# Moving two thirds of one layer's modulation from TensorE matmuls to VectorE row sums

## The chip, the cores and the metric

The kernel runs on one core of a Trainium2 chip. The metric is the device time of one execution in microseconds (us); smaller is better. Engines are named as in the profile: PE is TensorE's matmul (PEld its weight loads), DVE is VectorE, ACT is ScalarE, POOL is GpSimd, SP is SyncE, which here issues most of the DMAs.

## The reference

Two small models run one after the other on 256 tokens of width 1024. The first has two layers (convolution, pooling mixer, sparse attention, gated output). The second takes its output as a latent sequence x, adds a context sequence xc of 256 tokens, and has two layers of mixers (gated linear attention, short convolution, neighbourhood attention) and a convolutional FFN. Each layer of the second model is modulated by vectors that depend on the conditioning vectors c and c_ctx alone:

```python
for layer in range(DEPTH):                       # DEPTH = 2
    mod = silu(c) @ w_ada[layer] + b_ada[layer]        # 6 x 1024 values for the latent
    sh1, sc1, g1, sh2, sc2, g2 = split(mod, 6)
    modc = silu(c_ctx) @ w_ada[layer] + b_ada[layer]   # and 6 x 1024 for the context
    ...
    u = (rmsnorm(x) * (1 + sc1) + sh1) @ w_in[layer]
    x = x + g1 * (mixers(u) @ w_out[layer])
    h = rmsnorm(x) * (1 + sc2) + sh2
    x = x + g2 * conv_ffn(h)
    ...
```

The context goes the same way in layer 0, with modc; in layer 1 only its input to the mixers is needed. All is f32. A layer's w_ada has 1024 x 6144 values, 24 MB; nothing but c and c_ctx is needed to use it, so this product can be done at any time before its sixths are used.

## The kernel before, in words

Activations lie feature-major: 128 features on the partitions, tokens along the free axis. Weights come as units of 128 x 1024 f32 (512 KB), loaded by SP in the order of their use (`rawunit`, L425) into 4 buffers. `unit` (L437 and L445) splits a unit into a high and a low part, the high one by a copy on ACT, the low one by a subtraction on DVE, into 4 buffers, and `mm3` (L384 to L386) makes each product in three matmuls. `ftile` (L381 with `raw` operands) is the plain f32 form that some tiles take. A product's sum lies in one of 3 PSUM banks called mm; short chains (attention, norms, scans) use 4 banks called ax, and one bank is called ada.

The program is written as a main line of such tiles. Side work is written as Python generators: `tick` calls them, so that the main line's tiles and the side work's instructions alternate in program order, and a scheduler of the framework then fixes each engine's order, by program order and what is ready in its own model. A tick also calls `feed`, which takes `pace` steps of one more generator, `s.fill`. That is where the modulation is done:

- **`ada(0)`**, layer 0, inside the first model's layer 0: six rounds (a sixth of the 6144 columns each) of eight steps. A step loads 512 KB of w_ada into one of 4 buffers (L630) and issues four f32 matmuls with a stationary operand of 32 columns (silu of c and c_ctx in the first two), one for each quarter of the bank's partitions. Each shows as two instructions, so that one step is a group of 8 in the trace. At the end of a round ACT copies the bank out, and `turn` transposes it on PE (L619) and adds the bias on DVE. 48 steps and 6 turns, one step per tick.
- **`ada_rows(1)`**, layer 1, inside layer 0's FFN of the second model: c and c_ctx are spread over the partitions (one DMA of 1 MB, L651) and put through silu; then for each of 48 blocks of 128 features a load of 512 KB of the transposed w_ada into one of 2 buffers (L661) and a multiply-and-sum along the row on DVE (L664) with a read of its accumulator into `mod`. Blocks 0 to 15 are summed for context (j = 1) and latent (j = 0), blocks 16 to 47 for the latent only: 3 steps of preparation and 64 row sums, at 1.7 steps for each FFN pair (PAIR_PACE) and 2.5 for each tile of the down projection.

`mod[i]` has 48 columns per layer: 0 to 15 are sh1 and sc1, 16 to 23 g1, 24 to 39 sh2 and sc2, 40 to 47 g2. `norm2` uses columns 0 to 15 before the mixers and 24 to 39 before the FFN; `residual` uses 16 to 23 after the mixers and 40 to 47 after the FFN.

Order of the second model's layer 0 (`layer2`): `norm2` of latent and context; `mixers` (projections with the scan's and the attention's side work between them, then the output projection in three loops of 8 tiles: the part from scan and convolution for all tokens, then the attention's part for the context, then for the latent, with `norm2` for the FFN behind each of the last two); `ffn` (13 pairs of up projections, first half of the down projection, 9 pairs, second half). In layer 0's mixers before, `s.fill` is empty.

Of the kernel before, what the change touches and what calls it, by code (L numbers as in the profile page):

```python
# [8 lines left out]
F32 = mybir.dt.float32  # L9
# [14 lines left out]
PAIR_PACE = 1.7  # L24
# [16 lines left out]
ADA_PIN = 48  # L41
# [275 lines left out]
def layout(a):  # L317
    a = {k: np.asarray(v) for k, v in a.items()}
    d = {}
    units = []  # L320
    sp1 = []
    tokb = []
    for i in range(DEPTH):
        units += block1_units(i, a)
        sp1.append(block1_small(i, a))
        tokb.append(np.concatenate([a["b_in"][i][TOKC], a["b_in"][i][rng(V, 512)]]))
    d["units1"] = np.stack(units)
    d["sp1"] = np.stack(sp1)
    d["sw1"] = np.stack([block1_small_w(i, a) for i in range(DEPTH)])
    d["tokb"] = np.stack(tokb)  # L330
    d["xT"] = fm(a["x"][0].T, rng(0, T))
    d["pT"] = np.stack([fm(a["p"][i, 0].T, rng(0, T)) for i in range(DEPTH)])
    d["units2"] = np.stack([u for i in range(DEPTH) for u in block2_units(i, a)])
    d["sp2"] = np.stack([block2_small(i, a) for i in range(DEPTH)])
    d["wg2"] = np.stack([gate_weights(i, a) for i in range(DEPTH)])
    d["nab"] = np.stack([na_bias(i, a) for i in range(DEPTH)])
    d["wada"] = a["w_ada_2"][0].reshape(8, 128, 6144)

    d["wadaT"] = a["w_ada_2"][1].T.reshape(48, 128, 1024)
    d["crow"] = np.stack([a["c_2"][0], a["c_ctx_2"]]).reshape(1, 2 * D)  # L340
    d["cc"] = np.stack([colvec(a["c_2"][0]), colvec(a["c_ctx_2"])], 2).reshape(128, 16)
    d["ctxT"] = fm(a["ctx_2"][0].T, rng(0, T))
    d["c2"] = consts2()
    d["c0"] = consts0()
    d["c1"] = consts1()
    return {k: np.ascontiguousarray(v) for k, v in d.items()}
# [3 lines left out]
class Prog:  # L350
    def __init__(s, ctx, tc, A, out, dbg=None):
# [12 lines left out]
        s.turns = False  # L364
        s.inner = 0
# [242 lines left out]
    def ada(s, i):  # L608
        nc, A = s.nc, s.A
        pool = s.tmp  # L610
        mod = s.const.tile([128, 48, 2], F32, name=s.nm("mod"), tag=f"mod{i}")
        s.mod.append(mod)
# [13 lines left out]
        for rd in range(6):  # L626
            ps = bank[:, rd % 2 * 256 : rd % 2 * 256 + 256]
            for k in range(KT):
                w = s.t([128, 1024], "wada", 4, pool=pool)
                (s.pin if rd * KT + k < ADA_PIN else lambda x: x)(nc.sync.dma_start(w, A["wada"][k, :, rd * 1024 : rd * 1024 + 1024]))  # L630
# [14 lines left out]
    def ada_rows(s, i, bufs, pool):  # L645
        nc, A = s.nc, s.A
        mod = s.const.tile([128, 48, 2], F32, name=s.nm("mod"), tag=f"mod{i}")
        s.mod.append(mod)
        bias = s.sp2[i]["ada"]
# [3 lines left out]
        th = s.t([128, D], "adaj", 1, pool=pool)  # L653
        for j in range(2):
            s.a(th, c[:, j], AF.Tanh, scale=0.5)
# [3 lines left out]
        for m in range(48):  # L659
            w = s.t([128, D], "wada", bufs, pool=pool)  # L660
            s.pin(nc.sync.dma_start(w, A["wadaT"][m]))  # L661
            for j in (1, 0) if m < 16 else (0,):
                out = s.t([128, D], "adaj", 1, pool=pool) if j else w
                nc.vector.tensor_tensor_reduce(out=out, in0=w, in1=c[:, j], scale=1.0, scalar=bias[:, m : m + 1],  # L664
                                               op0=ALU.mult, op1=ALU.add, accum_out=mod[:, m, j : j + 1])
                yield 0

# [543 lines left out]
    def ffn(s, i, both, c0, n):  # L1211
# [28 lines left out]
        if both:  # L1240
            s.fill, s.pace = s.ada_rows(i + 1, 2, s.mx), PAIR_PACE
# [54 lines left out]
    def mixers(s, i, both, c0, n):  # L1296
# [3 lines left out]

        v = s.big([128, 4, 384], "A")
# [109 lines left out]
        st = [{}, {}]  # L1411
        for m in range(KT):
            s.residual(i, m, wtile(range(5), 0, m, c0, n), 16, c0, n, st, False)
            s.tick(NA_TICK)
        for j in (1, 0) if both else (0,):
# [12 lines left out]
            if both:  # L1428
                s.norm2(i, 1, s.rows(st[j]), j)
# [322 lines left out]
```

## Time and profile before

| | us |
|---|---|
| median of 3 runs (range) | 1469.65 (1467.91 to 1471.45) |
| the profiled execution | 1469.05 |
| its span, first to last instruction | 1467.2 |
| PE busy in it | 1403.8 (96%) |
| PEld busy | 1196.6 (82%) |
| DVE busy | 1057.1 (72%) |
| ACT busy | 695.6 (47%) |
| POOL busy | 160.3 (11%) |

The mean granted TensorE clock is 0.979 of full speed. The profiled execution lies 1.85 us above its own span and 0.6 us below the median of the runs. Layer 0 of the first model fills the span up to about 242 us and layer 1 up to about 420; the second model's layer 0 has its mixers from about 430 to 687 us and its FFN from there to about 1085; layer 1 fills the rest. A share of busy time is a mean over these stages, so each stage is read by itself: which engine has no idle time in it, and what ends the waits of the engines that do. A row of idle time says who released the engine; idle time of an engine that isn't the bound costs nothing.

### The profile page before, as it was taken

To read this page: it belongs to the slowest core of one execution; us is meant where nothing else is said; L and a number is where in the kernel's file an instruction comes from. 1 tells how busy PE (TensorE), PEld (TensorE's weight loads), DVE (VectorE), ACT (ScalarE), POOL (GpSimd) and SP (SyncE) were. 2 spreads that over 40 slices of the span, in tenths; PEclk is the share of its full clock that TensorE was granted. 3 is DMA by queue.
4 is the path that set the end of the run, shared out by engine and by line. 5 is a ranking of instruction groups with operands and counts; after the bars stand their busy time and mean duration, and the time that the engine had idled before them with its cause. 6 is when DMAs were issued, how large, how long until landed. Compare 5 with 4: busy or idle time off the path is not lost.

```text
span 1467.2 us, 25799 instructions
## 1 busy us (share of the span) xinstructions
PE 1403.8 (96%) x10178; PEld 1196.6 (82%) x10178; DVE 1057.1 (72%) x2128; ACT 695.6 (47%) x1294; POOL 160.3 (11%) x176
## 2 busy tenths in 40 slices
PE   8889999689999999999999999999999999999997
PEld 7657688677997877768888888888898887999997
DVE  6895656996976655465898886787367665698694
ACT  4635655636765233454444422343246245476562
POOL 1840001920020000002100000000210000100001
PEclk9999999999999999999999999999999999999998
DMA  7677685343452211112353565555333233376662
GB/s 263 249 254 263 206 310 187 101 144 115 135 172 86 88 59 55 58 55 101 89 183 117 164 223 201 171 186 174 89 97 101 87 97 92 108 211 195 185 197 77
DMA packets 63761, 218.02 MB, mean 149 GB/s; under 512 B 7254, under 2 KB 12312, under 8 KB 63512
## 3 DMA queue, kind: packets, MB, share of 16 engines
q1 hardware_dynamic: 58224, 208.17, 44.7%
q10 hardware_dynamic: 5416, 8.20, 1.8%
q8 instruction: 80, 1.31, 0.4%
q14 instruction: 41, 0.34, 0.1%
HBM read 215.30 MB, written 1.05 MB: 147 GB/s over the span
## 4 chain that ended last, share of the span: by engine, by line
PE 79%; DVE 9%; POOL 4%; issue 3%; ACT 3%; DMA 2%; ACTq 0%; POOLq 0%; DVEq 0%; SPq 0%
PE mm L384 21%; PE mm L385 21%; PE mm L386 21%; PE ax L381 10%; DVE hl L445 3%; POOL acc L943 2%; PE mm L381 2%; PE ada L381 2%; DMA raw<-in_units_dram 1%; DVE acc L392 1%; PE ax L1705 1%; ACT hl L437 1%; POOL sqa L526 1%; DVE isc L392 1%; DVE xx L392 1%
## 5 line engine op out<-in xcount | busy, mean ns | idle before, releaser
L384 PE MATMUL mm<-xx,hl 128*128 128x256 f32 (+1 forms) x1720 | 557.9, 326 | 16.2 <-ACT qr L405 7.6
L386 PE MATMUL mm<-xx,hl 128*128 128x256 f32 (+1 forms) x1720 | 549.0, 320 | 4.9 <-DVE hl L445 4.9
L385 PE MATMUL mm<-xx,hl 128*128 128x256 f32 (+1 forms) x1720 | 549.7, 320 | 0.0
L445 DVE TENSOR_TENSOR hl<-raw,hl 128x1024 fp32r<-128x1024 f32 x286 | 359.2, 1256 | 107.4 <-ACT hl L437 104.2
L437 ACT ACTIVATE hl<-raw 128x1024 fp32r<-128x1024 f32 x286 | 301.0, 1054 | 172.9 <-PE mm L386 151.3
L384 PEld LDWEIGHTS mm<-xx,hl 128*128 128x128 f32 x1720 | 328.4, 191 | 60.5 <-issue 13.1
L386 PEld LDWEIGHTS mm<-xx,hl 128*128 128x128 f32 x1720 | 328.7, 191 | 32.2 <-DVE hl L445 6.3
L385 PEld LDWEIGHTS mm<-xx,hl 128*128 128x128 f32 x1720 | 328.9, 192 | 29.7 <-issue 6.3
L392 DVE SCALAR_TENSOR_TENSOR y<-mm,sp,y 128x255 f32<-128x255 f32 (+1 forms) x184 | 109.1, 595 | 25.8 <-ACT y L405 24.3
L384 PE MATMUL mm<-hid,hl 128*128 128x256 f32 (+1 forms) x374 | 123.0, 329 | 0.0
L385 PE MATMUL mm<-hid,hl 128*128 128x256 f32 (+1 forms) x374 | 123.0, 329 | 0.0
L386 PE MATMUL mm<-hid,hl 128*128 128x256 f32 (+1 forms) x374 | 122.7, 328 | 0.0
L405 ACT ACTIVATE y<-mm,sp 128x256 f32<-128x256 f32 (+1 forms) x92 | 60.4, 657 | 116.2 <-PE mm L386 116.0
L526 POOL TENSOR_TENSOR sqa<-sqa,sq 128x256 f32<-128x256 f32 x36 | 32.1, 896 | 690.5 <-ACT sq L405 689.8
L384 PEld LDWEIGHTS mm<-hid,hl 128*128 128x128 f32 x374 | 70.5, 188 | 7.2
L385 PEld LDWEIGHTS mm<-hid,hl 128*128 128x128 f32 x374 | 70.5, 188 | 7.1
L386 PEld LDWEIGHTS mm<-hid,hl 128*128 128x128 f32 x374 | 70.5, 188 | 6.9
L392 DVE SCALAR_TENSOR_TENSOR x<-mm,mod,x 128x256 f32<-128x256 f32 x96 | 43.5, 478 | 44.2 <-PE mm L386 44.0
L385 PE MATMUL mm<-hl,xx 128*128 128x416 f32 (+3 forms) x192 | 68.4, 356 | 5.2 <-DVE hl L445 5.2
L664 DVE CUSTOM_DVE_ANT_0 wada<-wada,crow,sp 128x1024 f32<-128x1024 f32 x48 | 61.0, 1280 | 11.1 <-DMA wada<-in_wadaT_dram 10.8
L384 PE MATMUL mm<-hl,xx 128*128 128x416 f32 (+3 forms) x192 | 68.1, 356 | 0.4 <-DVE glr L1306 0.2
L386 PE MATMUL mm<-hl,xx 128*128 128x416 f32 (+3 forms) x192 | 67.1, 350 | 0.0
(279 smaller groups left out, 1752.1 us busy)
## 6 DMA issues: line engine op xcount, KB each, us to landing
raw<-in_units_dram SPq DMA_DIRECT2D x296, 512.0 KB, 3.7
wada<-in_wada_dram SPq DMA_DIRECT2D x48, 512.0 KB, 4.9
wada<-in_wadaT_dram SPq DMA_DIRECT2D x48, 512.0 KB, 4.6
nab<-in_nab_dram ACTq DMA_DIRECT2D x12, 192.0 KB, 2.5
x<-in_xT_dram SPq DMA_DIRECT2D x4, 256.0 KB, 5.2
x<-in_ctxT_dram ACTq DMA_DIRECT2D x1, 1024.0 KB, 6.6
crow<-in_crow_dram SPq DMA_DIRECT2D x1, 1024.0 KB, 6.6
c<-in_c_dram ACTq DMA_DIRECT2D x1, 928.0 KB, 5.2
```

The source lines that it names most:

```text
L381: return s.nc.tensor.matmul(out, lhsT, rhs, start=start, stop=stop, **kw)
L384: s.nc.tensor.matmul(out, l[0], r[0], start=start, stop=False)
L385: s.nc.tensor.matmul(out, l[0], r[1], start=False, stop=False)
L386: s.nc.tensor.matmul(out, l[1], r[0], start=False, stop=stop)
L392: s.nc.vector.scalar_tensor_tensor(out, a, sc, b, op0, op1)
L405: s.nc.scalar.activation(out, in_, func, bias=bias, scale=scale)
L437: a = nc.scalar.activation(hl[:, 0], raw, AF.Copy)
L445: b = nc.vector.tensor_sub(hl[:, 1], raw, hl[:, 0].bitcast(F32))
L526: (eng or s.nc.vector).tensor_tensor(st["acc"], st["acc"], sq, ALU.add)
L664: nc.vector.tensor_tensor_reduce(out=out, in0=w, in1=c[:, j], scale=1.0, scalar=bias[:, m : m + 1], op0=ALU.mult, op1=ALU.add, accum_out=m ...
L943: nc.gpsimd.tensor_tensor(acc[:, j], acc[:, j], pr, ALU.add)
L1705: nc.tensor.transpose(pt[:, kt * 128 : kt * 128 + 128], L[j][:, kt * 128 : kt * 128 + 128], s.ident)
```

## The change

`ada(0)` keeps its first two rounds (sh1 and sc1, `ADA_PE = 2`): 16 steps and 2 turns stay on PE in the first model, 32 steps and 4 turns go. `ada_rows` takes a list of (layer, block) and is used twice. In layer 0's mixers it does blocks 16 to 39 of layer 0, for context and latent, at 0.8 steps per tick (3 steps of preparation, 48 row sums). In layer 0's FFN it does blocks 40 to 47 of layer 0 and then the 48 blocks of layer 1 (3 steps and 80 row sums), at 2.0 steps per pair. Before the output projection the generator is run on until g1 is there; before `norm2` for the FFN it is run to its end. A context row sum (j = 1) is now two instructions of 512 columns that write their products to the PSUM bank ada, the second starting from the first one's sum, so that no SBUF buffer is needed for them. A context row sum is one step, as before. The DMA scratch setting at the foot makes room in SBUF.

```diff
-PAIR_PACE = 1.7
+PAIR_PACE = 2.0
...
-ADA_PIN = 48
+ADA_PE = 2
+ADA_MIX = range(16, 40)
+MIX_PACE = 0.8
...
-    d["wada"] = a["w_ada_2"][0].reshape(8, 128, 6144)
-
-    d["wadaT"] = a["w_ada_2"][1].T.reshape(48, 128, 1024)
+
+    d["wada"] = a["w_ada_2"][0][:, : ADA_PE * 1024].reshape(8, 128, ADA_PE * 1024)
+    d["wadaT"] = a["w_ada_2"].transpose(0, 2, 1).reshape(DEPTH, 48, 128, 1024)
...
-        for rd in range(6):
+        for rd in range(ADA_PE):
...
-                (s.pin if rd * KT + k < ADA_PIN else lambda x: x)(nc.sync.dma_start(w, A["wada"][k, :, rd * 1024 : rd * 1024 + 1024]))
+                s.pin(nc.sync.dma_start(w, A["wada"][k, :, rd * 1024 : rd * 1024 + 1024]))
...
-    def ada_rows(s, i, bufs, pool):
+    def ada_rows(s, todo, bufs, pool):
...
-        th = s.t([128, D], "adaj", 1, pool=pool)
         for j in range(2):
+            th = s.t([128, D], "wada", bufs, pool=pool)
...
-        for m in range(48):
+        for i, m in todo:
+            mod, bias = s.mod[i], s.sp2[i]["ada"]
             w = s.t([128, D], "wada", bufs, pool=pool)
-            s.pin(nc.sync.dma_start(w, A["wadaT"][m]))
-            for j in (1, 0) if m < 16 else (0,):
-                out = s.t([128, D], "adaj", 1, pool=pool) if j else w
-                nc.vector.tensor_tensor_reduce(out=out, in0=w, in1=c[:, j], scale=1.0, scalar=bias[:, m : m + 1],
-                                               op0=ALU.mult, op1=ALU.add, accum_out=mod[:, m, j : j + 1])
+            s.pin(nc.sync.dma_start(w, A["wadaT"][i, m]))
+            for j in (1, 0) if m < 16 or i < DEPTH - 1 else (0,):
+                if j:
+
+                    out, b = s.bank("ada"), bias[:, m : m + 1]
+                    for h in range(2):
+                        c_ = slice(h * 512, h * 512 + 512)
+                        nc.vector.tensor_tensor_reduce(out=out, in0=w[:, c_], in1=c[:, j, c_], scale=1.0, scalar=b,
+                                                       op0=ALU.mult, op1=ALU.add, accum_out=mod[:, m, j : j + 1])
+                        b = mod[:, m, j : j + 1]
+                else:
+                    nc.vector.tensor_tensor_reduce(out=w, in0=w, in1=c[:, j], scale=1.0, scalar=bias[:, m : m + 1],
+                                                   op0=ALU.mult, op1=ALU.add, accum_out=mod[:, m, j : j + 1])
                 yield 0
+            if (i, m) == (0, 23):
+                s.gated = True
...
         if both:
-            s.fill, s.pace = s.ada_rows(i + 1, 2, s.mx), PAIR_PACE
+            s.fill = s.ada_rows([(0, m) for m in range(40, 48)] + [(1, m) for m in range(48)], 2, s.mx)
+            s.pace = PAIR_PACE
...
+        if both:
+            s.fill, s.pace = s.ada_rows([(0, m) for m in ADA_MIX], 2, s.mx), MIX_PACE
         v = s.big([128, 4, 384], "A")
...
         st = [{}, {}]
+        while both and not s.gated:
+            next(s.fill)
         for m in range(KT):
             s.residual(i, m, wtile(range(5), 0, m, c0, n), 16, c0, n, st, False)
             s.tick(NA_TICK)
+        s.pace = MIX_PACE
...
             if both:
+                for _ in s.fill:
+                    pass
                 s.norm2(i, 1, s.rows(st[j]), j)
...
-    nc = _bacc.Bacc("TRN2", target_bir_lowering=False, num_devices=1)
+    nc = _bacc.Bacc("TRN2", target_bir_lowering=False, num_devices=1, dynamic_dma_scratch_size=1024)
```

## Rows read from the trace of the kernel before

**Rows 1.** The page: busy time by engine, the chain that ended last.

```profile
PE 1403.8 (96%) x10178; PEld 1196.6 (82%) x10178; DVE 1057.1 (72%) x2128; ACT 695.6 (47%) x1294; POOL 160.3 (11%) x176
PE 79%; DVE 9%; POOL 4%; issue 3%; ACT 3%; DMA 2%; ACTq 0%; POOLq 0%; DVEq 0%; SPq 0%
```

**Rows 2.** The chain that ended last, 107 to 242 us: shares by line.

```profile
by line: PE mm L384 18.1%; PE mm L385 15.8%; PE mm L386 15.6%; PE ada L381 15.0%; PE ax L381 14.2%; PE mm L381 10.1%; PE ax L1094 2.5%; PE ax L384 2.5%; PE ax L385 1.4%; PE ax L386 1.4%; PE ax L619 1.1%; ACT aPT L405 0.7%; POOL clr L508 0.6
```

**Rows 3.** Busy time by window: length, PE, PEld, DVE, ACT, POOL; clock, DMA.

```profile
107.00:242.00 135.00, 133.54 (x1121) 105.28 (x1122) 81.12 (x200) 71.28 (x164) 1.63 (x2) 1.00 0.73 243
173.00:190.00 17.00, 17.00 (x162) 12.51 (x163) 10.96 (x22) 7.03 (x13) 0.00 (x0) 1.00 0.78 258
```

**Rows 4.** Groups by line, 107 to 242 us, PE: the modulation's matmuls and transposes.

```profile
L381 PE MATMUL ada<-wada,cs 128*32 128x256 f32 x280 | 22.8, 391 | 0.0
...
L619 PE MATMUL ax<-c,adae 128*128 128x128 f32 x8 | 1.8, 301 | 0.0
```

**Rows 5.** Timeline of PE around single steps of the modulation (start, duration).

```profile
154.06 0.64 PE L381 MATMUL ada<-wada,cs 128*32 128x256 f32 x8
154.63 0.44 PE L1094 MATMUL ax<-c,aL 128*128 128x128 f32 x2
...
190.86 0.28 PE L385 MATMUL mm<-xx,hl 128*128 128x256 f32 x1
190.97 0.28 PE L386 MATMUL mm<-xx,hl 128*128 128x256 f32 x1
191.18 0.64 PE L381 MATMUL ada<-wada,cs 128*32 128x256 f32 x8
191.75 0.39 PE L384 MATMUL ax<-qi,hl 128*128 128x256 f32 x1
191.98 0.28 PE L385 MATMUL ax<-acc,hl 128*128 128x256 f32 x1
```

**Rows 6.** Groups by line and form, DVE: row sums, preparation, a 512-column form on PSUM.

```profile
L664 DVE CUSTOM_DVE_ANT_0 wada<-wada,crow,sp 128x1024 f32<-128x1024 f32 x48 | 61.0, 1280 | 11.1 <-DMA wada<-in_wadaT_dram 10.8
...
L664 DVE DVE_READ_ACCUMULATOR2_ANT mod<- 128x1 f32 x64 | 5.2, 82 | 0.0
...
L392 DVE SCALAR_TENSOR_TENSOR crow<-adaj,crow 128x1024 f32<-128x1024 f32 x2 | 2.8, 1382 | 0.9 <-ACT crow L405 0.7
...
L401 DVE TENSOR_TENSOR scp<-mm,slO 128x512 f32<-128x512 f32 x2 | 1.4, 690 | 4.7 <-PE mm L386 4.7
```

**Rows 7.** Busy time by window, layer 0's mixers, their end, the FFN's beginning.

```profile
430.00:626.00 196.00, 193.70 (x1691) 154.12 (x1692) 113.49 (x301) 80.56 (x166) 10.02 (x11) 0.97 0.24 70
626.00:687.00 61.00, 58.26 (x341) 43.34 (x341) 34.67 (x89) 29.46 (x74) 5.30 (x6) 0.98 0.28 93
687.00:705.00 18.00, 14.86 (x90) 14.03 (x91) 13.39 (x29) 8.99 (x18) 5.41 (x7) 0.78 0.00 1
705.00:722.00 17.00, 15.54 (x120) 15.21 (x120) 14.63 (x33) 7.58 (x17) 1.62 (x1) 0.90 0.33 94
```

**Rows 8.** Waits of PE in the mixers, 430 to 668 us: total, times, longest.

```profile
PE ax L1621 <- DVE slO L401: 1.5, 1, 1.5
PE ax L1705 <- DVE slA L396: 1.1, 2, 0.5
```

**Rows 9.** Timeline of DVE at the context's norm, 691 to 694 us.

```profile
691.02 0.87 DVE L392 SCALAR_TENSOR_TENSOR nf<-x,modA,ax 128x256 f32<-128x256 f32 x2 [1.22 <-PE ax L381]
...
692.30 1.27 DVE L664 CUSTOM_DVE_ANT_0 adaj<-wada,crow,sp 128x1024 f32<-128x1024 f32 x1
```

**Rows 10.** The page, DMA issues: count, KB each, median us to landing.

```profile
wada<-in_wadaT_dram SPq DMA_DIRECT2D x48, 512.0 KB, 4.6
```

**Rows 11.** Busy time by window, layer 0's FFN: pairs of the first half, then the rest.

```profile
722.00:850.00 128.00, 128.00 (x584) 104.73 (x584) 115.20 (x168) 55.54 (x74) 0.00 (x0) 1.00 0.50 156
850.00:1050.00 200.00, 200.00 (x859) 161.33 (x858) 141.45 (x202) 66.58 (x83) 5.11 (x6) 1.00 0.55 179
```

**Rows 12.** Busy time by window, the tile ada alone, sum over 107 to 242 us.

```profile
sum 135.00, PE 22.78 PEld 5.75 ACT 1.88; mean PE 4.56 PEld 1.15 ACT 0.38
```

More of the change, by code (lines that the diff above doesn't have):

```diff
@@ L364, in __init__ @@
         s.turns = False
+        s.gated = False
         s.inner = 0
@@ L610, in ada @@
         pool = s.tmp
-        mod = s.const.tile([128, 48, 2], F32, name=s.nm("mod"), tag=f"mod{i}")
-        s.mod.append(mod)
+        for d in range(DEPTH):
+            s.mod.append(s.const.tile([128, 48, 2], F32, name=s.nm("mod"), tag=f"mod{d}"))
+        mod = s.mod[i]
         bias = s.sp2[i]["ada"]
@@ L641, in ada @@
         turn(*prev)
-    def ada_rows(s, i, bufs, pool):
+    def ada_rows(s, todo, bufs, pool):
         nc, A = s.nc, s.A
-        mod = s.const.tile([128, 48, 2], F32, name=s.nm("mod"), tag=f"mod{i}")
-        s.mod.append(mod)
-        bias = s.sp2[i]["ada"]
         c = s.t([128, 2, D], "crow", 1, pool=pool)
```

## The prediction, made before the changed kernel was run

> **What bounds the kernel now.** I read the page first. PE is busy for 96% of the span, DVE for 72%, and 79% of the chain that ended last runs on PE [rows 1]. A mean over stages decides nothing, so I went to the stage that loses work and then to the one that gains it.
>
> The stage that loses is layer 0 of the first model, 107 to 242 us. Before 107 us 13 of the 48 steps have run; the first 16 stay, so 32 of the 35 steps in this stretch go. Here PE is busy 133.5 of 135 us at the full clock (1.00, that is 2.4 GHz), DVE 81 and ACT 71 [rows 3]. The chain runs through PE almost wholly, and 15.0% of it, 20.2 us, are the modulation's matmuls, 1.1% its transposes [rows 2]. So PE is the bound here and these steps lie on its path.
>
> The stage that gains is layer 0's mixers and FFN. From 430 to 626 us PE is busy 193.7 of 196 us and DVE 113.5 [rows 7]; all that PE waits for DVE up to 668 us is 2.6 us [rows 8]. In the FFN's first pairs PE has no idle time and DVE is already busy 115.2 of 128 us [rows 11]. PE is the bound again, and DVE has room that differs by stretch.
>
> **What leaves PE.** 280 instructions are 35 groups of 8, 22.8 us busy [rows 4]. A busy time of overlapping matmuls is no price, so I take starts. Between split matmuls the last one starts at 190.97, the group at 191.18, the next at 191.75 and the one behind it at 191.98: 0.78 and 0.23 where two usual spacings are 0.11 each [rows 5], so a group costs 0.67 + 0.12 = 0.79. Between other f32 matmuls only the 0.57 from 154.06 to 154.63 counts [rows 5]. I put 20 groups at 0.79 and 12 (the attention's stretch and the layer's end) at 0.57: 15.8 + 6.8 = 22.6 us. Four turns with two transposes each, 1.8 us busy for four [rows 4], give 1.5 more. Together 24 us, the most there is to win. Not all of it will come: from 173 to 190 us eight groups leave 17.0 − 8 × 0.79 = 10.7 us of PE work beside 10.96 of DVE [rows 3], so DVE binds there next, and in the attention the chain over ACT and DVE shows. I take off 3: **−21 us**, with 20 to 24 as bounds (20 is the chain's own figure). The four copies on ACT, eight small additions on DVE and 32 loads on SP that go with them free nothing that binds here; they only bring the units' loads earlier.
>
> There is a rule that speaks against this reading. In this stretch the weight loads fill only 105.3 of the 135 us [rows 3]. The Trainium skill, Perfetto Trace Analysis, section Identifying the Most-Contended Engine, says that a matmul's busy share is a bad measure of how near PE is to its limit and that the share of the weight loads should be taken. By that PE would stand at 78% here and would not be the bound, and the sum below would begin with −5 in place of −21. The starts do not agree with it: they follow each other without a gap, and the group's 0.79 us is a spacing [rows 5]. I go by the starts and keep a PE that isn't the bound as a rival.
>
> **What comes to DVE.** A latent row sum is 1.28 us and its accumulator read 0.08 [rows 6]: 1.36. The trace has no row sum of 512 columns that writes to PSUM. Its bounds are half of the long form, 0.64, and no gain from the shortening, 1.28; I take 0.69, the 512-column form with an operand in PSUM [rows 6], which is nearest in size and memory. Two halves and two reads are 1.54, a block with both sums 2.90.
>
> - Mixers: 24 blocks, 69.6 us, and two preparations of 1.38 [rows 6] on DVE: 72.4 us. ACT gets four passes more of about a us each in a stretch where it is busy 80.6 of 196 us [rows 7], hidden. The upper bound of the half adds 48 × 0.59 = 28 us.
> - FFN: 8 blocks, 23.2, and 16 context sums of layer 1 that are now halves, 16 × 0.18 = 2.9: 26.1 us.
>
> **What of it shows.** Where do the steps fall? Counted in the code, layer 0's mixers have 36 ticks ahead of the output projection, then 8, 8 and 8. At 0.8 a tick that is 28 steps by the beginning of the output projection, which I put at 626 us, 13 more in the two loops that follow, and the last 10 of the 51 at one go before the context's `norm2`.
>
> - Up to 626 us: 3 steps of preparation and 25 of 1.45 us on the mean, 39 us into 82.5 us of idle DVE [rows 7]. DVE goes from 58 to 78%. At 90% it still costs PE nothing in the FFN's pairs [rows 11], which gives a lower bound of 0; but the scan's and the attention's chains alternate between PE and DVE, and each can wait for a row sum that has just begun. In the one short stretch with DVE at 86% and chains of norms, PE lost 1.5 of 17 us [rows 7], 9%, which makes 17 us of 196: the upper bound. Between the two I take the value near the FFN and near the 2.6 us that PE waits now [rows 8]: **+3 us**.
> - 626 to 687 us: 23 steps, 33.4 us, into 26.3 us of idle DVE [rows 7]: 7.1 us too much. What is queued behind it: columns 24 to 39 must be there before `norm2` of the context, which began about 691.0 us [rows 9], and the FFN's first tiles wait for that. Some of it will be done earlier, since a row sum needs only its load, and SP runs ahead: the first row sum of layer 1 ran at 692.3 [rows 9], long before the third pair's tick, where the code has it. The lower bound is 0. The upper bound is that nothing runs ahead: five blocks at one go through two buffers, each 4.6 us to land [rows 10] and 2.9 to sum, 5 × 7.5 / 2 = 19 us. I take **+5 us**.
> - SP: 24 loads and the 1 MB of c now stand among the units' loads, and one that waits for its buffer holds the units behind it. Eight units (four raw, four split) cover that, and the DMA engines are busy 24% there [rows 7]: 0. If that cover is gone, PE waits for a unit, which counts in the 17 us above. POOL's queue is passed by nothing.
> - FFN: at 2.0 steps a pair in place of 1.7 the first pairs get some 5 sums more and 14 split ones, 6.8 + 2.5 = 9.3 us into 12.8 idle [rows 11]; the rest has 58.6 idle. **+1 us**, bounds 0 and 9.
>
> Sum: −21 + 3 + 5 + 1 = −12. The profiled execution took 1469.05 us, 1.85 more than its span and 0.6 less than the median of the runs; 1469.05 − 12 = **1457 us**. With 20 to 24 won and 3 to 18 given back the case's own range is 1447 to 1467.
>
> **The rivals.**
>
> - *All row sums hidden.* For it: no idle PE at 90% DVE in the pairs [rows 11]. Against it: the 7.1 us too much before the FFN. 1469 − 24 = 1445.
> - *The norm's gate.* The last five blocks run at one go, the FFN starts 19 us later: −21 + 19 + 4 = +2, 1471. For it: the loop that empties the generator right ahead of `norm2`, PE already short there (14.9 of 18 us, 1.5 of 17 lost behind it) [rows 7]. Against it: the row sum at 692.3 [rows 9].
> - *DVE's order becomes the bound in the mixers.* A row sum cannot be interrupted; if half of the 72 us stand in front of a scan or attention step that PE waits for, the mixers grow by 36 us: 1469 − 21 + 36 + 1 = 1485. It decides from 20 us on, 28% of the row sums' time. Against it: 82.5 us of idle DVE up to 626 and three mm banks that feed PE meanwhile; for it: what PE waits for now are just such steps, the scan's sum and the attention's scaling [rows 8].
> - *PE was not the bound in the first model.* Then what goes is only the weight loads' share. The stretch has 35 steps with 5.75 us of these loads [rows 12]; 32 of them are 5.3 us: 1469 − 5 + 9 = 1473. Against it: the chain and the starts [rows 2, 5]. The Trainium skill, Perfetto Trace Analysis, section Identifying the Most-Contended Engine, is the rule that would lead here.
>
> That the change doesn't do what it says can hardly be: the 32 groups are out of the code.
>
> **How the numbers follow.** A measurement of this kernel can tell about 0.2%, 2.9 us. Chances: forecast 0.66, all hidden 0.14, the norm's gate 0.08, DVE's order 0.07, PE not the bound 0.05. Faster: 0.66 + 0.14 = 0.80; same: 0.08; slower: 0.07 + 0.05 = 0.12. The range takes in the forecast's own, the hidden case at 1445 and the gate at 1471, and leaves out 0.12 and a part of the forecast's tail.
>
> **What would show it.** Right: layer 0 of the first model ends 20 to 24 us earlier, at about 221 us, and layer 1 is shifted whole; 16 groups of modulation matmuls on PE; the halves at 0.69 us; DVE near 80% up to the output projection, PE's waits for DVE up by 3 us there; 5 us more between the last context tile and the FFN's first pairs. Wrong: an idle PE in 107 to 221 us with DMA or DVE as the releaser; PE waits for DVE of more than 20 us in the mixers, or a lower granted clock there; `norm2` of the context later than the shift allows by 10 us and more.

## The result, and the profile after

The changed kernel takes 1458.59 us (median of 4 runs, 1456.47 to 1459.71), the kernel before 1470.55 us on the same chip (4 runs, 1467.91 to 1474.62): a ratio of 0.9915, 95% interval 0.9888 to 0.9941. That is faster by more than the 0.2% that can be told, and 1.6 us above the forecast of 1457. The profiled execution took 1457.7 us with a span of 1455.9 us, against 1469.05 and 1467.2.

The page of the changed kernel, busy time by engine and the chain that ended last, answers to [rows 1]:

```profile
PE 1395.0 (96%) x9914; PEld 1197.0 (82%) x9914; DVE 1142.1 (78%) x2346; ACT 696.3 (48%) x1294; POOL 164.1 (11%) x176
PE 74%; DVE 11%; POOL 4%; issue 4%; DMA 3%; ACT 3%; ACTq 0%; POOLq 0%; DVEq 0%; SPq 0%
```

PE has lost 264 matmuls and DVE has 85 us more to do. PE is still busy for 96% of a shorter span. The groups by line and form, the modulation's matmuls and the row sums (count, busy us, mean ns), answer to [rows 4, 6]:

```profile
L384 PE MATMUL ada<-wada,cs 128*32 128x256 f32 x128 | 10.7, 406 | 5.1 <-ACT adae L408 5.1
...
L674 DVE CUSTOM_DVE_ANT_0 wada<-wada,crow,sp 128x1024 f32<-128x1024 f32 x80 | 101.8, 1280 | 5.4 <-DMA wada<-in_wadaT_dram 4.8
L670 DVE CUSTOM_DVE_ANT_0 ada<-wada,crow,mod 128x512 f32<-128x512 f32 x48 | 36.2, 754 | 0.7
L670 DVE CUSTOM_DVE_ANT_0 ada<-wada,crow,sp 128x512 f32<-128x512 f32 x48 | 36.1, 752 | 3.6 <-DMA wada<-in_wadaT_dram 3.3
L670 DVE DVE_READ_ACCUMULATOR2_ANT mod<- 128x1 f32 x96 | 13.2, 138 | 0.1
```

128 matmuls, 16 groups, are left. A half row sum into PSUM takes 0.75 us and its read 0.14.

Busy time by window of the changed kernel (length; PE, PEld, DVE, ACT, POOL busy with counts; granted clock, DMA share, GB/s), cut where about the same work stands (to within 2 us), answers to [rows 3, 7, 11]:

```profile
107.00:222.00 115.00, 114.45 (x893) 101.33 (x892) 80.62 (x194) 69.52 (x159) 1.79 (x2) 1.00 0.45 142
410.00:616.70 206.70, 203.59 (x1692) 160.96 (x1693) 158.09 (x405) 83.97 (x170) 11.30 (x11) 0.93 0.33 112
616.70:678.30 61.60, 60.65 (x350) 43.84 (x349) 53.24 (x133) 29.38 (x75) 5.09 (x6) 1.00 0.42 135
690.30:708.80 18.50, 13.87 (x81) 13.46 (x82) 15.96 (x36) 6.68 (x16) 1.62 (x1) 0.73 0.28 86
708.80:841.20 132.40, 132.40 (x618) 108.26 (x617) 125.74 (x213) 56.84 (x77) 0.00 (x0) 1.00 0.49 159
```

The first line is where the time comes from: 115 us for what took 135. The second is where it goes: the mixers up to the output projection took 196 us before. DVE stands at 76% there, near the 78% forecast, and PE idles 3.1 us where it idled 2.3. So PE does not wait more. What differs is the granted clock, 0.93 where [rows 7] has 0.97.

Where does the gain stand at each point? The timeline of DVE, the context's first gated tile, the first copy of the mixers, the first residual sums of the output projection and of the down projection (start, duration), before:

```profile
341.80 0.48 DVE L392 SCALAR_TENSOR_TENSOR nf<-x,modA,rctx 128x256 f32<-128x256 f32 x1
...
430.01 0.18 DVE L1306 COPY glr<-mm 128x32 f32<-128x32 f32 x1
...
629.86 0.88 DVE L392 SCALAR_TENSOR_TENSOR x<-mm,mod,x 128x256 f32<-128x256 f32 x2 [0.15 <-PE mm L386]
...
860.52 0.48 DVE L392 SCALAR_TENSOR_TENSOR x<-mm,mod,x 128x256 f32<-128x256 f32 x1
```

And after:

```profile
321.85 0.48 DVE L395 SCALAR_TENSOR_TENSOR nf<-x,modA,rctx 128x256 f32<-128x256 f32 x1
...
409.98 0.17 DVE L1321 COPY glr<-mm 128x32 f32<-128x32 f32 x1
...
620.55 0.48 DVE L395 SCALAR_TENSOR_TENSOR x<-mm,mod,x 128x256 f32<-128x256 f32 x1
...
851.66 0.48 DVE L395 SCALAR_TENSOR_TENSOR x<-mm,mod,x 128x256 f32<-128x256 f32 x1
```

20.0 us are won in the first model and kept up to the mixers; the mixers give back 10.7, the stretch behind them 0.4; the rest of the span wins some 2, and 11.3 are left.

### The profile page after: what moved, and what is told of

It is laid out like the page before. It is cut to its first block, busy times and chain, and to the rows that moved or that the text cites. A ratio compares the mean times of both kernels' runs of the same rounds, so it can differ in the third digit from the quotient of the medians.

```text
span 1455.9 us, 25470 instructions
## 1 busy us (share of the span) xinstructions
PE 1395.0 (96%) x9914; PEld 1197.0 (82%) x9914; DVE 1142.1 (78%) x2346; ACT 696.3 (48%) x1294; POOL 164.1 (11%) x176
## 4 chain that ended last, share of the span: by engine, by line
PE 74%; DVE 11%; POOL 4%; issue 4%; DMA 3%; ACT 3%; ACTq 0%; POOLq 0%; DVEq 0%; SPq 0%
PE mm L387 20%; PE mm L388 20%; PE mm L389 20%; PE ax L384 10%; DVE hl L448 3%; POOL acc L955 3%; DMA wada<-in_wadaT_dram 2%; PE mm L384 1%; DMA raw<-in_units_dram 1%; PE ax L1725 1%; ACT hl L440 1%; DVE wada L674 1%; DVE acc L395 1%; PE ada L384 1%; DVE xx L395 1%
## 5 line engine op out<-in xcount | busy, mean ns | idle before, releaser
L387 PEld LDWEIGHTS mm<-xx,hl 128*128 128x128 f32 x1720 | 329.5, 192 | 56.3 <-issue 11.3
L674 DVE CUSTOM_DVE_ANT_0 wada<-wada,crow,sp 128x1024 f32<-128x1024 f32 x80 | 101.8, 1280 | 5.4 <-DMA wada<-in_wadaT_dram 4.8
```

Of the source, the lines that this page charges most:

```text
L387: s.nc.tensor.matmul(out, l[0], r[0], start=start, stop=False)
L674: nc.vector.tensor_tensor_reduce(out=w, in0=w, in1=c[:, j], scale=1.0, scalar=bias[:, m : m + 1], op0=ALU.mult, op1=ALU.add, accum_out=mod ...
```

## The experiments

Kernels of one group shared a chip and its runs of the kernel before. I call three stretches by these marks: *first model* (0 to the first gated tile), *mixers* (first copy to the first output-projection sum) and *behind* (from there to the first down-projection sum). **Lost to the clock** is here, but for one table of all runs, (1 − granted clock) × 4 us summed over slices of 4 us. It is what the slices would have been shorter at 2.4 GHz if PE set the pace in all of them, so rather an upper bound.

### First group: what is won, what is given back, and a late load

`gain_only` leaves all first-layer row sums out:

```diff
-ADA_MIX = range(16, 40)
+ADA_MIX = range(0)
...
+        s.nc.gpsimd.memset(mod[:, ADA_PE * 8 :], 0.5)
...
-            s.fill = s.ada_rows([(0, m) for m in range(40, 48)] + [(1, m) for m in range(48)], 2, s.mx)
+            s.fill = s.ada_rows([(1, m) for m in range(48)], 2, s.mx)
```

> The changed kernel without its 40 blocks of first-layer row sums (24 in the mixers, 16 in the FFN; the pair pace is back at 1.7): those columns of the modulation hold a constant, so that part of the computation is left out. Theory (TensorE sets the pace of the first model, and all that is given back comes from the row sums later): the gates of the first norm come about 20 us earlier than before (322 against 342 us in the trace), as in the changed kernel; the mixers keep this gain up to the first out-projection sum (610 against 630 us, where the changed kernel has 620.6), and the whole is 1445 to 1450 us. Rival 1 (TensorE is not the bound of the first model, and the 11 us of the changed kernel are all that there is): about 1458 us, as the changed kernel. Rival 2 (the gain is lost by a clock that is granted less often when TensorE is denser, whatever VectorE does): the gates at 322 us, the first sum at 618 to 621 us, the whole 1456 to 1459 us.

It took 1447.2 us, ratio 0.9859 (0.9836 to 0.9882). The gates (the first gated tile) come at 322.3 us and the total lies in the theory's range, so the gain of the first model is real and worth 20 us by itself. But the first output-projection sum comes at 615.1 us, not 610: 4.4 us of it go in the mixers without one row sum there. The theory of the time was incomplete; rival 2, the clock, has a part in this trace. The profiled execution was the slowest of the five (1453.61 us, mean granted clock 0.975, the others 0.978 to 0.983), so its trace shows more loss than an average run has.

`prefetch` was aimed at a stall that I had seen in the trace of the changed kernel, on DVE's timeline:

```profile
493.35 0.76 DVE L670 CUSTOM_DVE_ANT_0 ada<-wada,crow,sp 128x512 f32<-128x512 f32 x1 [2.13 <-DMA wada<-in_wadaT_dram]
```

The scan's mask copies stand behind this row sum on DVE, PE waits 0.8 us for the tile that they fill (AT) at 496.6 us, and slow matmuls follow. The edit issues each load one block ahead:

```diff
+        def load():
+            if todo[len(got) :]:
+                i, m = todo[len(got)]
+                got.append(m)
+                ws.append(s.t([128, D], "wada", bufs, pool=pool))
+                s.pin(nc.sync.dma_start(ws[-1], A["wadaT"][i, m]))
...
         for i, m in todo:
-            w = s.t([128, D], "wada", bufs, pool=pool)
-            s.pin(nc.sync.dma_start(w, A["wadaT"][i, m]))
+            load()
+            w = ws.pop(0)
```

> The changed kernel with each block's load issued one block ahead of its row sums (two tiles as before); nothing is left out. Theory (late load): the wait of 2.1 us at 493 us shrinks to under 0.5 us, the slow clock behind it goes, the first out-projection sum comes at 613 to 616 us and the whole takes 1450 to 1453 us. Rival 1 (the load of VectorE as such): 1457 to 1460 us. Rival 2 (the loads' issues wait on SP's queue for the tile to come free, and hold back what stands behind them): another transfer comes late, TensorE waits elsewhere, 1458 to 1464 us.

The wait at that place is now 0.63 us, as DVE's timeline of this kernel shows:

```profile
492.46 0.76 DVE L681 CUSTOM_DVE_ANT_0 ada<-wada,crow,sp 128x512 f32<-128x512 f32 x1 [0.63 <-DMA wada<-in_wadaT_dram]
```

Yet the first output-projection sum comes at 621.0 us, and the whole takes 1462.26 us, ratio 0.9947 (0.9929 to 0.9966). The late load was a good story and it fell: what comes behind it comes without it. The total is in rival 2's range, but its reason does not show in the mixers, where PE idles 3.6 us here and 3.3 in the changed kernel; 3.7 us more are behind the mixers.

`late_fill` is the kernel before with layer 1's row sums begun later:

```diff
-            s.fill, s.pace = s.ada_rows(i + 1, 2, s.mx), PAIR_PACE
+            rows, s.pace = s.ada_rows(i + 1, 2, s.mx), PAIR_PACE
...
                     for j in js[:2]:
                         pair(j, a, T, us[j])
+                if both:
+                    s.fill, s.pace = rows, PAIR_PACE + 0.5
```

> The kernel before, in which the second layer's row sums and their preparation start only after the first four half-pairs of the FFN, at a pace of 2.2 in place of 1.7; nothing is left out. Theory (the transition from the mixers to the FFN became 4 to 6 us shorter in the changed kernel because no preparation and no row sum stands between the steps of the norms on VectorE): the time from the first out-projection sum to the first gated tile of the FFN falls from 90.1 us to 84 to 87 us, and the whole takes 1464 to 1467 us. Rival (the transition is shorter for another reason, such as the clock): 89 to 91 us, the whole 1468 to 1472 us.

1466.54 us, ratio 0.9975 (0.9955 to 0.9995). From the first output-projection sum to the first gated tile it took 83.5 us where 84 to 87 were expected and 90.1 stood before. So row sums and preparation between the steps of the norms do cost. Of the 7 us that the whole stretch behind the mixers gains, 5.2 are granted clock in these two profiles (lost there: 6.9 before, 1.7 here). The whole kernel won 0.25%, 3.7 us, and this profile is of one of its faster runs (1462.88 us).

### Second group: which row sums cost, the loads, and the same kernel again

`mix_only` has the mixers' blocks alone, `ffn_only` the FFN's alone; in each the other blocks' columns hold a constant, by the edits of `gain_only` on one half.

> The changed kernel with only the mixers' 24 blocks of first-layer row sums; the FFN's eight are left out, their columns of the modulation hold a constant, and the pair pace is back at 1.7. The kernel with none of the 40 blocks took 1447.2 us, the changed one 1458.6 us: 11.4 us to share out. Theory now (the mixers' sums cost 5 to 8 us, by short waits on VectorE and one more fall of the granted clock, the FFN's 3 to 5 us by the denser pairs): 1453 to 1456 us, the first out-projection sum at 618 to 621 us. Rival 1 (the FFN's part carries nearly all): 1447 to 1450 us. Rival 2 (the mixers' part carries nearly all): 1457 to 1459 us.

1459.09 us, ratio 0.9922 (0.9893 to 0.995), first sum at 618.2 us: nearly all of the cost, rival 2.

> The changed kernel with only the FFN's eight blocks of first-layer row sums at pair pace 2.0; the mixers' 24 are left out, their columns hold a constant. Theory: the first out-projection sum at 613 to 617 us as with no row sums at all (615.1), the time from the first gated FFN tile to the first down-projection sum 2 to 5 us longer than the 143.7 us of that kernel, the whole 1450 to 1453 us. Rival 1 (the FFN carries nearly all): 1456 to 1459 us. Rival 2 (the mixers carry nearly all): 1446 to 1449 us.

1455.19 us, ratio 0.990 (0.9859 to 0.9941), first sum at 614.6 us, as the theory had it, and 148.9 us from the first gated FFN tile to the first down-projection sum, 5.1 more than in `gain_only`. By its total this one lies between the theory and rival 1, and its total and that of `mix_only` do not add up to the 11.4 us. The intervals are 7 to 12 us wide, so I read the traces' stretches from here on and not the differences of totals.

`resident2` takes away every load but the first in the mixers:

```diff
+            if (i, m) in [(0, q) for q in ADA_MIX] and still is not None:
+                w = still
+            else:
...
+                if m in ADA_MIX and i == 0:
+                    still = w
+                    junk = s.t([128, D], "wada", bufs, pool=pool)
...
-                    nc.vector.tensor_tensor_reduce(out=w, in0=w, in1=c[:, j], scale=1.0, scalar=bias[:, m : m + 1],
+                    nc.vector.tensor_tensor_reduce(out=w if still is None else junk, in0=w, in1=c[:, j], scale=1.0, scalar=bias[:, m : m + 1],
```

> The changed kernel in which the mixers' 24 blocks are all summed from the first block's tile, with a second tile for the products: VectorE does every row sum, no row sum after the first waits for a load, and 23 loads of 0.5 MB are left out with their share of the queue; 23 blocks' sums are of the wrong weights. The kernel with loads one block ahead has shown that the wait of 2.1 us at 493 us alone is not what costs (first out-projection sum 621.0 us without it). Theory now (VectorE's in-order time is what costs, and the loads cost nothing): first sum at 619 to 622 us, the whole 1456 to 1460 us. Rival (the loads cost, by the transfers and by issues that stand ahead of the kernel's weight loads on SP's queue): first sum at 614 to 617 us, the whole 1450 to 1454 us.

1464.68 us, ratio 0.9963 (0.994 to 0.9986), first sum at 621.2 us. The loads cost the mixers nothing: without them these take 212.5 us, no less than with them. That the total came out above both ranges I did not expect; the stretch behind the mixers is 1 us longer than in the changed kernel's two profiles, and what follows it 2 to 6 us.

> The changed kernel once more, unaltered, beside the three runs above. If the granted clock falls at the same places in every execution of one program, the profile shows falls near 460, 496 to 512 and 576 to 592 us again and a loss against full clock of 12 to 15 us between 400 and 640 us (13.6 us in the first profile). If the falls come by chance, their places in the second half of the mixers differ, and the loss differs by 3 us or more. The whole 1456 to 1460 us either way.

1459.46 us, ratio 0.9938 (0.9915 to 0.9962). Its profile, against the first one, is the turning point. Granted clock in slices of 4 us (columns as above), the changed kernel first:

```profile
492.00:496.00 4.00, 3.80 (x24) 2.84 (x22) 2.56 (x8) 1.36 (x2) 0.00 (x0) 1.00 0.81 326
496.00:500.00 4.00, 3.41 (x49) 2.91 (x50) 4.00 (x14) 0.64 (x3) 0.00 (x0) 0.66 0.29 90
500.00:504.00 4.00, 4.00 (x32) 3.19 (x32) 3.00 (x7) 0.38 (x2) 0.00 (x0) 0.50 0.37 132
504.00:508.00 4.00, 4.00 (x33) 3.23 (x32) 1.45 (x6) 0.80 (x2) 0.00 (x0) 0.50 0.56 180
508.00:512.00 4.00, 4.00 (x12) 3.13 (x12) 3.18 (x8) 0.00 (x0) 1.95 (x1) 0.63 0.00 0
```

The same program again:

```profile
496.00:500.00 4.00, 3.96 (x52) 2.82 (x52) 4.00 (x12) 0.56 (x2) 0.00 (x0) 0.66 0.41 131
500.00:504.00 4.00, 4.00 (x33) 3.23 (x32) 2.33 (x4) 0.28 (x1) 0.00 (x0) 0.50 0.43 138
504.00:508.00 4.00, 4.00 (x33) 3.23 (x32) 2.26 (x8) 0.80 (x2) 0.00 (x0) 0.50 0.36 128
508.00:512.00 4.00, 4.00 (x13) 3.14 (x12) 2.79 (x7) 0.00 (x0) 2.33 (x1) 0.63 0.00 0
```

And `gain_only`, without one row sum in the mixers:

```profile
492.00:496.00 4.00, 4.00 (x37) 3.13 (x38) 1.59 (x6) 1.54 (x2) 0.00 (x0) 1.00 0.01 4
496.00:500.00 4.00, 4.00 (x73) 3.27 (x66) 1.87 (x5) 0.83 (x3) 0.00 (x0) 0.70 0.28 78
500.00:504.00 4.00, 4.00 (x33) 3.23 (x32) 1.29 (x5) 0.68 (x2) 0.00 (x0) 0.50 0.14 57
504.00:508.00 4.00, 4.00 (x11) 3.13 (x10) 1.28 (x3) 0.13 (x1) 1.32 (x1) 0.52 0.00 0
508.00:512.00 4.00, 4.00 (x32) 3.25 (x31) 1.49 (x4) 1.54 (x2) 0.00 (x0) 1.00 0.00 0
```

Two executions of one program fall at the same place by the same amount: (0.34 + 0.50 + 0.50 + 0.37) × 4 = 6.8 us lost. In the mixers it is no chance of one run. And the fall comes without row sums too, a little shorter, with PE busy all of 492 to 496 us, and of the 56 us before them at full clock but for 0.02 us. PE's timeline of `gain_only` shows what it did before:

```profile
495.26 0.66 PE L384 MATMUL ax<-bigA,AT 128*128 128x64 f32 x4
495.85 0.53 PE L384 MATMUL ax<-gU,gq 32*32 32x64 f32 x20
...
497.36 0.90 PE L384 MATMUL ax<-bigA,AT 128*128 128x64 f32 x4
```

In the kernel before, the same work 17.7 us later ran on at full clock:

```profile
512.99 0.66 PE L381 MATMUL ax<-bigA,AT 128*128 128x64 f32 x4
513.58 0.53 PE L381 MATMUL ax<-gU,gq 32*32 32x64 f32 x20
...
515.09 0.66 PE L381 MATMUL ax<-bigA,AT 128*128 128x64 f32 x4
```

Its window, and the fall in `ffn_only`, the other kernel with the shift and no row sums in the mixers:

```profile
512.00:516.00 4.00, 4.00 (x86) 3.50 (x85) 2.80 (x7) 2.00 (x4) 0.00 (x0) 1.00 0.03 6
...
496.00:500.00 4.00, 4.00 (x33) 3.33 (x33) 0.16 (x1) 0.56 (x2) 0.00 (x0) 0.50 0.51 135
```

So in both kernels starting the mixers earlier was by itself enough to move where the clock falls. Whether it also costs anything is for all runs to tell, below. The Trainium skill, TensorE: Matmul & The Clock Gate, section HAM oscillation, tells of a kernel whose clock falls in its waits for DMA; here the rows show a fall with no wait ahead of it.

### The account of all profiles

Length, what of it is lost to the clock, and the difference (us), from one profile each:

```
                  mixers                behind               first model
               length lost  rest    length lost  rest    length lost  rest
before          199.9  5.1 194.7     230.7  6.9 223.8     341.8 12.0 329.8
late_fill       198.4  3.4 195.0     223.6  1.7 221.9     342.6 13.7 328.8
gain_only       204.3 10.2 194.1     229.0  3.4 225.5     322.3 17.0 305.2
ffn_only        204.0  8.6 195.4     231.5  3.4 228.1     321.9 15.4 306.5
mix_only        210.6 13.7 196.9     230.3  5.2 225.2     319.5 15.4 304.2
changed         210.6 13.6 196.9     231.1  5.1 226.0     321.9 17.0 304.9
after_again     212.3 15.4 196.9     231.3  5.2 226.1     319.4 13.7 305.6
prefetch        212.1 15.3 196.7     234.8  5.1 229.8     320.7 11.9 308.8
resident2       212.5 15.4 197.2     232.1  3.4 228.6     319.9 15.3 304.6
after_late      209.1 12.0 197.1     225.5  1.7 223.8     322.6 18.8 303.8
paced           208.8 12.0 196.8     234.4  5.2 229.3     321.8 15.4 306.4
ada3_late       210.1 13.7 196.4     221.5  0.0 221.5     325.8 13.6 312.2
paced_late      209.4 13.6 195.8     225.6  1.7 223.9     319.7 13.6 306.1
ada_second      209.9 12.0 198.0     224.9  1.7 223.2     321.8 17.0 304.8
```

Read the mixers' last column first. Four kernels without row sums there stand at 194.1 to 195.4 us, ten with them at 195.8 to 198.0: apart from the clock the row sums cost the mixers about 2 us, wherever they stand and whether their loads wait or not. The lengths differ by up to 14 us, and that is the middle column: 3.4 to 5.1 lost where the first model has its old length, 8.6 and 10.2 where it is shorter and the mixers have no row sums, 12.0 to 15.4 where they have. Up to 1440 us the changed kernel loses 37.5 us to the clock and the kernel before 27.4. Without that it would be 1467.2 − 27.4 = 1439.8 against 1455.9 − 37.5 = 1418.4: 21 us, of which the clock takes 10 back in these two profiles.

A profile is one run of several, and each run's span and mean granted clock are on record. Here (1 − mean clock) × span, the end of the kernel included, is averaged over all runs of a kernel and set beside the kernel before on the same chip in the same group; *rest* is the span less that (us):

```
              runs   lost  before     rest   before
gain_only       5    30.1   31.6    1416.2   1436.3
late_fill      12    31.9   31.6    1432.1   1436.3
ffn_only        4    33.4   30.2    1419.9   1436.6
mix_only        5    38.8   30.2    1418.3   1436.6
after_again    10    39.2   30.2    1418.6   1436.6
after_late      6    39.0   32.5    1415.0   1436.6
```

A difference of two lost figures is good to about 1.6 us, for `gain_only` 2.2 (standard errors). This corrects the reading of single profiles. The changed kernel wins 18.0 us apart from the clock and gives 9.0 back to it. Without row sums in the mixers the shift adds −1.5 and 3.3 us of loss over the whole span; with them it is 8.6 and 9.0. So the shift alone moves the falls from one stretch to another, and most of the added loss comes with the mixers' row sums. How they bring it on stays open: without the loads it was as large (40.2 us lost in `resident2`).

### Third and fourth group: can it be had back?

`after_late` puts `late_fill`'s step into the changed kernel, with the same edit at its place.

> The changed kernel in which the FFN's row sums and their preparation start only after the first four half-pairs, at a pace of 2.5 in place of 2.0; nothing is left out. In the kernel before the same step took 7 us out of the stretch from the first out-projection sum to the first down-projection sum (223.6 for 230.7 us), 5 of them of granted clock. Theory (what costs there is VectorE's preparation and row sums between the steps of the norms, and TensorE's idle time and clock behind them): the stretch falls from the changed kernel's 231.2 us to 224 to 228 us, the whole is 1452 to 1456 us. Rival (the changed kernel has that gain already, since its first row sum of the FFN comes only at 706 us): the stretch stays at 230 to 232 us, the whole at 1457 to 1460 us.

1456.54 us, ratio 0.990 (0.9877 to 0.9923), the stretch behind 225.5 us: the theory's stretch; the total is half a us above its range. Over all runs the late start wins about 4 us apart from the clock, here (1418.6 to 1415.0) as in `late_fill` (1436.3 to 1432.1), and nothing clear of the clock itself.

`paced` moves the mixers' row sums away from the crowded stretch at 450 to 460 us:

```diff
-            s.fill, s.pace = s.ada_rows([(0, m) for m in ADA_MIX], 2, s.mx), MIX_PACE
+            s.fill, s.pace = s.ada_rows([(0, m) for m in ADA_MIX], 2, s.mx), 0.4
...
         st8["chain"] = True
+        if both:
+            s.pace = 1.1
```

> The changed kernel with the mixers' pace at 0.4 up to the end of the scan's state chain and 1.1 from there to the out-projection, in place of 0.8 throughout; nothing is left out, the row sums are the same and only their places differ. In the changed kernel VectorE is busy 9.75 of the 10 us from 450 to 460 us, TensorE idles 1.1 us there, and the granted clock falls behind it. Theory (TensorE's waits behind a full VectorE bring on that fall): no fall near 460 us, a loss against full clock between 400 and 640 us of 8 to 11 us in place of 13.6 to 15.4, the first out-projection sum 3 to 5 us earlier against the start of the scan, the whole 1453 to 1456 us. Rival (the falls come with the shape of TensorE's own work and not with the row sums' places): a loss of 13 to 16 us, the whole 1457 to 1461 us.

1460.18 us, ratio 0.993 (0.9905 to 0.9955). Windows of the changed kernel:

```profile
452.00:460.00 8.00, 6.91 (x124) 5.41 (x124) 7.76 (x23) 4.13 (x9) 0.00 (x0) 0.98 0.19 69
460.00:464.00 4.00, 4.00 (x13) 3.15 (x12) 3.75 (x17) 0.00 (x0) 0.00 (x0) 0.61 0.00 0
```

and of `paced`:

```profile
452.00:460.00 8.00, 7.98 (x130) 6.54 (x129) 7.73 (x23) 4.22 (x9) 0.00 (x0) 1.00 0.41 133
460.00:464.00 4.00, 4.00 (x62) 3.04 (x62) 3.84 (x12) 0.48 (x1) 0.00 (x0) 1.00 0.01 2
564.00:572.00 8.00, 8.00 (x46) 6.42 (x46) 4.83 (x15) 1.78 (x4) 1.69 (x1) 0.58 0.32 121
```

PE's idle time and the fall near 460 are gone, as the theory said. But another fall stands at 564, and 12.0 us are lost in the mixers, between the theory's 8 to 11 and the rival's 13 to 16. In this trace taking PE's idle time away moved a fall more than it removed one. The rival has the total.

`ada3_late` leaves three rounds on PE (`ADA_PE = 3`, `ADA_MIX = range(24, 40)`), with the late start.

> The changed kernel with three of the six rounds of the first layer's modulation on TensorE in place of two, 16 blocks in the mixers in place of 24, and the FFN's row sums after the first four half-pairs; nothing is left out. Theory (a round costs the first model 5 us, and eight blocks fewer save the mixers 2 to 4 us): the gates of the first norm at 326 to 328 us, the mixers from the first gate to the first out-projection sum 206 to 209 us in place of 210.6, the whole within 2 us of the kernel with two rounds and the same late start. Rival 1 (the mixers' cost sets in only with the blocks ahead of the out-projection): the mixers at 204 to 205 us, the whole 2 to 4 us faster than that kernel. Rival 2 (the mixers' cost is the same with any row sums): 3 to 6 us slower.

1456.27 us, ratio 0.9908 (0.9883 to 0.9932): gates at 325.8 us, mixers 210.1 where the theory had 206 to 209. Eight blocks fewer save the mixers nothing, as rival 2 had it; the total is the theory's because the stretch behind, 221.5 us, loses nothing to the clock.

`paced_late` joins both steps.

> The changed kernel with both steps: the mixers' pace at 0.4 up to the end of the scan's state chain and 1.1 after it, and the FFN's row sums only after the first four half-pairs; nothing is left out. Alone, the first took 2 to 3 us out of the mixers and cost 3 us behind them, the second took 6 us out of the stretch behind the mixers. Theory (the two act in different stretches, and the 3 us behind the mixers were the FFN's preparation coming later): mixers 208 to 210 us, the stretch to the first down-projection sum 224 to 227 us, the whole 1453 to 1456 us. Rival (the row sums that the pacing moves past the scan crowd the steps before the norms, whatever the FFN does): the stretch 228 to 234 us, the whole 1457 to 1461 us.

1454.94 us, ratio 0.9899 (0.9872 to 0.9926), mixers 209.4 and the stretch behind 225.6 us: the theory in all three. It is the fastest version that computes all. It beats the kernel before clearly; against the changed kernel (0.9915 and 0.9938) the intervals overlap, so 2 to 6 us are likely, not settled.

`ada_second` is `after_late` with the two rounds that stay on PE fed in the first model's second layer:

```diff
-        s.pace = PACE[1]
+        s.pace = PACE[1] if i else 0
```

and so at the three places that follow.

> The kernel with the late start of the FFN's row sums, in which the two rounds of modulation that stay on TensorE are fed in the first model's second layer in place of its first; nothing is left out. In the changed kernel their 16 groups run from 45.9 to 119.3 us, and from 256 to 292 us, where the kernel before was at full clock up to 284 us, the granted clock falls. Theory (16 groups cost TensorE the same time wherever they stand, and where the clock falls in the first model is a matter of how the stretch lies, not of the row sums): the gates of the first norm at 318 to 325 us, the whole 1454 to 1458 us. Rival (the groups keep TensorE's clock up where its own work is thin): a loss against full clock in the first model of 10 to 13 us in place of 16 to 19, the gates at 314 to 318 us, the whole 1449 to 1453 us.

1459.52 us, ratio 0.992 (0.9891 to 0.995). The groups now run from 208.2 to 283.5 us; gates at 321.8 us, 17.0 us lost to the clock. Gates and clock are the theory's, the total lies 1.5 us above its range; in this trace the groups do not hold the clock up.

## Why the prediction was right, point by point

- **What leaves PE, −21.** Measured −20.0 and −22.4 us (`after_again`). Less the clock, an upper bound, the first model takes 303.8 to 308.8 us with two rounds, 328.8 and 329.8 with six: 20 to 26. Over all its runs `gain_only` has 20.0 apart from the clock. The 3 us taken off the gross 24 were put down to DVE and the attention's chain; the rows show PE busy 114.45 of 115 us in that stretch. So the sum was right and its reason was not; whether the group's price was too high or the clock took the 3 us (5.0 more lost in the first model, 1.7 the second time) is not settled.
- **PE was not the bound** (1473) is refuted. The rule of the Trainium skill, Perfetto Trace Analysis, section Identifying the Most-Contended Engine, would have led to −5; the trace disagrees with −20.0.
- **Half row sum, 1.54 for two.** The halves measure 0.75 each in place of 0.69, the reads 0.14 in place of 0.08. By starts (618.94 and 619.78, the next instruction at 620.55) a pair costs 1.61. The term was 0.07 us too low, and 48 of these are 3 us of DVE in all.
- **Mixers up to 626 us, +3.** This is the mis-sized term: 10.7 us, 12.4 the second time. As a price of waits behind DVE it was right: the rest column gives 2.2. What it lacked is the clock, +8.5 us, named among the signs of failure (a lower granted clock there) and given no term. In the profiles of `gain_only` and `ffn_only` 5.1 and 3.5 us of such a loss come in the mixers with the shift alone, but over the whole span of all runs the shift adds −1.5 and 3.3, and the mixers' row sums the greater part.
- **Transition +5, FFN +1.** Measured +0.4 together. The burst ahead of `norm2` did not come: the last of the mixers' row sums ended at 665.7 us, 12.6 us before the context's norm steps at 678.3. The step that failed is the count of code ticks, 28 steps up to 626 us: by 616.7 us, where the same work stands, 17 blocks with two sums each and the preparation had run, 37 steps. In the FFN DVE at 95% (125.74 of 132.40) cost PE no idle time.
- **DVE's order as the bound** (1485): PE idles 3.1 us in the mixers up to 616.7 us, and its waits for DVE from 410 to 650 us come to 2.2. Refuted.

So −21 + 3 + 5 + 1 = −12 came out as −20 + 10.7 + 0.4 − 2.4 = −11.3. The first term was right by its mechanism; that the total came within 2 us of the forecast is luck, since 7.7 us too little for the mixers and 5.6 us too much behind them cancelled. (By its own terms, 1469 − 24 + 3, the lower end of the case's range is 1448, not 1447.)

## What to carry to other kernels

When work is taken off an engine that sets the pace, cost what follows by its length at full clock and its granted clock apart: here 18 us were won apart from the clock and 9 given back to it, most of it with the row sums that went into the mixers. Read the clock's share from all runs: a shift of 20 us alone moved the falls, and the profile that showed 5 us lost in the mixers by it was of the slowest of five runs. Before a stall seen in a trace is mended, look whether what follows it also stands in a kernel without it. Fill work on DVE did better outside the chain of the norms: begun after the FFN's first half-pairs it made that stretch 7.1 us shorter in the kernel before and 5.6 in the changed one, by single profiles, and some 4 us apart from the clock over all runs.

## What the runs showed of the hardware that was not expected

The granted clock fell from 2.4 to 1.2 GHz with PE busy without a gap (4.00 of 4.00 us, then 0.70 and 0.50), and from 496 us to the end of the mixers at the same places by the same amounts in two executions of one program, even though the second had been 2.0 us ahead at the mixers' beginning. In the first model the two differ (17.0 and 13.7 us lost), and the mean clock of the changed kernel's 14 runs goes from 0.970 to 0.976. The second's first sum came only 0.3 us earlier: a fall near 460 us took the lead away. What decides where a fall comes and how long it lasts stays open; no run here moved only that. Open too is why `prefetch`, `resident2` and `paced` take some 3 us more behind the mixers apart from the clock (228.6 to 229.8 against 226.0); in all three, and in `ffn_only` (228.1), the FFN's eighth gated tile comes 52 us after the fourth, in the changed kernel 47, and no experiment took that apart.
